# Where the gate decays are subtracted, and when a head's last transposes are issued, in a fused hybrid layer

## The chip, the core and the metric

One core of a Trainium2 chip. The core has five engines, each with a queue of its own that it works through in order: TensorE (PE, matrix multiply), VectorE (DVE), ScalarE (ACT), GpSimd (POOL) and SyncE (SP, which here only issues transfers). The metric is device time in microseconds, the median of a few runs.

## The reference

The kernel computes one decoder layer in float32 on 1024 positions of width 1024. All branch inputs come from one projection `z = h W_in` with `h = rmsnorm(x)`. Branch A is a chunked gated unit. Branch B, in which the change lies, is gated linear attention with 4 heads (key width 128, value width 256) in chunks of 64 positions:

```python
log_a = log_sigmoid(b_lr @ w_a2 + b_a2) / 16
b = cumsum(log_a within a chunk);  b_last = b[63];  b_ref = b[31]
qe = q * exp(b - b_ref);  ke = k * exp(b_ref - b)
o_intra = tril(qe ke^T) v
chunk_kv = (k * exp(b_last - b))^T v;  decay = exp(b_last)
state = decay * state + chunk_kv            # over the chunks
o = o_intra + (q * exp(b)) state_before
y = x + rmsnorm(concat(a_out, rmsnorm(o) * silu(b_gate)) @ W_out)
```

So each gate needs four exponentials: of b, of b less the middle of its chunk (d below) with both signs (the negative one is ke), and of the chunk's last value less b (f below).

## The kernel before, in words

Every float32 operand of a large product is split into a rounded high part and a low part (`split`, L106: a cast on ScalarE, L108, and a subtraction, L109, on VectorE or GpSimd), and a product is three matmuls (`mm3`, L114 to L116). The stages follow one another on TensorE: normalisation and the first projections (to about 72 us), the gated linear attention (about 72 to 316, with a tail), the projections of branch A, and the output projection.

For a head, `qk` (L441) runs over two halves of 512 positions. For each half `gates` (L394) makes the decays: one small matmul (L397), log-sigmoid in three ScalarE and two VectorE operations (L405 to L413), the cumulative sum b on VectorE (L415), d on VectorE (L420), f on GpSimd (L424), and four exponentials on ScalarE (ke L428, d L429, b L430, f L431), of which three overwrite their input. Then the key and query projections (`proj_col`) are multiplied by the four (L448 to L457), and the chunk products follow (`products`, L462). There are eight gates: four heads, two halves. After `qk`, a head projects its values and gates token tile by token tile (`proj_tok`), and `attend` (L485) makes the output of one tile: scaled on VectorE (L516, L520), two tiles together transposed on TensorE (L527), copied on ScalarE (L528), and after every fourth tile stored to `mix_d` by a transfer that GpSimd issues (L534).

What sets the order: closures are put off with `later(fn, n)` (L75); every four steps of a projection's inner dimension, `tick()` counts all of them down and issues those that are due. One such step is twelve matmuls of 512 columns. A tile pair's transposes (`out`, L522) are put off by 3 steps, the last pair of a head by 4 (L538); they then fall into the next head's `qk`, or, for the last head, into the projections of branch A. Within this program order a planner, which simulates the engines with a cost model, lays out each engine's queue: among the instructions that it believes ready it takes them by priority. So an edit in one place can change the queues of all engines. `issue_after(x)` makes the instructions of its block follow x on their engine. Tiles of a pool share their buffers in turn: f, b, d, ke and m have one buffer each, projection results take turns on eight PSUM banks. Between the projections and other work, the sums of `w_out` blocks for the output stage (`wout_sums`, L217) are made on VectorE (L230), from blocks loaded by SyncE, and stored back by it. After the last head, `vn` (L584) takes the memory of the closed pools; ScalarE evacuates the value projections into it (L656), and L662 transposes another weight in two banks.

Of the kernel before, what the change touches and what calls it, by code (L numbers as in the profile page):

```python
# [11 lines left out]
AF = mybir.ActivationFunctionType  # L12
ALU = mybir.AluOpType
PSUM = bass.MemoryType.PSUM

P = 128
S = 1024
D = 1024
NT = S // P
# [5 lines left out]
CH = 64  # L25
TAU = 16.0
# [7 lines left out]
def hybrid_layer(  # L34
# [16 lines left out]
    nc = tc.nc  # L51
    x, out = x[0], out[0]
# [16 lines left out]
    def bank():  # L69
        return psum.tile([P, 512], F32, tag="ps", name="ps")  # L70
# [4 lines left out]
    def later(fn, n=1):  # L75
        pending.append([n, fn])
# [19 lines left out]
    def rsqrt(dst, mean, more=None):  # L96
        if more is None:
            nc.gpsimd.tensor_scalar(out=dst, in0=mean, scalar1=EPS, scalar2=None, op0=ALU.add)
        else:
            nc.gpsimd.tensor_scalar(  # L100
                out=dst, in0=mean, scalar1=EPS, scalar2=more, op0=ALU.add, op1=ALU.add
            )
        nc.gpsimd.tensor_tensor(out=dst, in0=dst, in1=neghalf[:, : dst.shape[-1]], op=ALU.pow)


    def split(hi, lo, src, eng=None):  # L106

        cast = nc.scalar.copy(out=hi, in_=src)  # L108
        return cast, (eng or nc.vector).tensor_tensor(out=lo, in0=src, in1=hi.bitcast(F32), op=ALU.subtract)  # L109

    def mm3(ps, a, b, start, stop, goes_on=False):

        how = {"skip_group_check": True} if goes_on else {}
        nc.tensor.matmul(ps, a[0], b[0], start=start, stop=False, **how)  # L114
        nc.tensor.matmul(ps, a[0], b[1], start=False, stop=False, **how)  # L115
        nc.tensor.matmul(ps, a[1], b[0], start=False, stop=stop, **how)  # L116
# [217 lines left out]
    with tc.tile_pool(name="gla", bufs=1) as gp:  # L334
# [3 lines left out]
            out=causal, in_=causal, pattern=[[1, P]], base=0, channel_multiplier=-1,  # L338
# [11 lines left out]
        for i in range(4):  # L350
# [4 lines left out]
            out=w2[32:64], in0=w2_raw[32:64], in1=w2[32:64].bitcast(F32), op=ALU.subtract  # L355
# [8 lines left out]
        for r, w in enumerate(w_lr):  # L364
            nc.gpsimd.memset(w.bitcast(F32), 0.0)
            src = lr_raw[:, 4 * r : 4 * r + 4]
            for i in (0, 1, 3):
                nc.scalar.copy(out=w[:, :, 32 * i : 32 * i + RANK], in_=src)
            nc.gpsimd.tensor_tensor(
                out=w[:, :, 64 : 64 + RANK], in0=src, in1=w[:, :, 0:RANK].bitcast(F32), op=ALU.subtract  # L370
# [4 lines left out]
        for hf in range(2):  # L375
# [3 lines left out]
            for k in range(KT):  # L379
# [7 lines left out]
                out=lrT[96:128, c], in0=pl[96:128], in1=lrT[96:128, c].bitcast(F32), op=ALU.subtract  # L387
            )

        tt = nc.vector.tensor_tensor  # L390
# [3 lines left out]
        def gates(hd, hf):  # L394

            pz = bank()
            nc.tensor.matmul(  # L397
                pz, w2[:, hd * DK : (hd + 1) * DK], lrT[:, hf * 512 : (hf + 1) * 512],
                start=True, stop=True,
            )  # L400
            bias = ba[:, hd : hd + 1]

            f = gp.tile([P, 8, CH], F32, tag="f", name="f")
            sp = f.rearrange("p n c -> p (n c)")
            nc.scalar.activation(out=sp, in_=pz, func=AF.Abs, bias=bias)  # L405
            m = gp.tile([P, 8, CH], F32, tag="m", name="m")
            mf = m.rearrange("p n c -> p (n c)")
            nc.vector.tensor_scalar(
                out=mf, in0=pz, scalar1=bias, scalar2=0.0, op0=ALU.add, op1=ALU.min
            )  # L410
            nc.scalar.activation(out=sp, in_=sp, func=AF.Exp, scale=-1.0)
            nc.scalar.activation(out=sp, in_=sp, func=AF.Ln, bias=1.0)
            tt(out=mf, in0=mf, in1=sp, op=ALU.subtract)  # L413
            b = gp.tile([P, 8, CH], F32, tag="b", name="b")
            nc.vector.tensor_tensor_scan(  # L415
                out=b.rearrange("p n c -> p (n c)"), data0=seg, data1=mf, initial=0.0,
                op0=ALU.mult, op1=ALU.add,
            )
            d = gp.tile([P, 8, CH], F32, tag="d", name="d")
            tt(  # L420
                out=d, in0=b, in1=b[:, :, CH // 2 - 1 : CH // 2].to_broadcast([P, 8, CH]),
                op=ALU.subtract,
            )
            nc.gpsimd.tensor_tensor(  # L424
                out=f, in0=b[:, :, CH - 1 : CH].to_broadcast([P, 8, CH]), in1=b, op=ALU.subtract
            )
            ke = gp.tile([P, 8, CH], F32, tag="ke", name="ke")
            nc.scalar.activation(out=ke, in_=d, func=AF.Exp, scale=-1.0 / TAU)  # L428
            nc.scalar.activation(out=d, in_=d, func=AF.Exp, scale=1.0 / TAU)  # L429
            nc.scalar.activation(out=b, in_=b, func=AF.Exp, scale=1.0 / TAU)  # L430
            nc.scalar.activation(out=f, in_=f, func=AF.Exp, scale=1.0 / TAU)  # L431
            dec = gp.tile([P, LINE, 1], F32, tag="dec", name="dec", bufs=2)[:, 0:8]
            nc.vector.tensor_copy(dec, b[:, :, CH - 1 : CH])
            dec2 = gp.tile([P, LINE, 1], F32, tag="dec2", name="dec2", bufs=3)[:, 0:4]
            tt(out=dec2, in0=dec[:, 0::2], in1=dec[:, 1::2], op=ALU.mult)
            return b, d, f, ke, dec, dec2, m

        def parts(tag, shape, bufs):
            return [gp.tile(shape, F32R, tag=tag + i, name=tag + i, bufs=bufs) for i in "hl"]
# [45 lines left out]
        def attend(hd, t, got, v, sg, cur):  # L485

            qsp, kst, sc, dec2 = got[t // 4]
            j = t % 4
            po = bank()
            o = po[:, 0:DV]  # L490
            prev = cur.get("parts")
            if t < NT - 1:
                pn = bank()[:, 0:DV]
                mm3(pn, [k[:, j] for k in kst], v, True, True)
                if t == 0:
                    cur["st"] = gp.tile([P, DV], F32, tag="st", name="st")
                    nc.vector.tensor_copy(cur["st"], pn)
                else:
                    stt(
                        out=cur["st"], in0=cur["st"], scalar=dec2[:, j], in1=pn,  # L500
                        op0=ALU.mult, op1=ALU.add,
                    )
                cur["parts"] = parts("st", [P, DV], 2)
                split(*cur["parts"], cur["st"])
            mm3(o, [s[:, j] for s in sc], v, True, t == 0)
            if t > 0:
                mm3(o, [q[:, j] for q in qsp], prev, False, True)
            e = t % 2
            if e == 0:
                cur["og"] = gp.tile([P, 2, DV], F32, tag="og", name="og", bufs=2)  # L510
                cur["oss"] = gp.tile([P, LINE], F32, tag="oss", name="oss", bufs=2)[:, 0:2]
            og, oss = cur["og"], cur["oss"]
            nc.scalar.activation(
                out=og[:, e], in_=o, func=AF.Square, scale=DV ** -0.5, accum_out=oss[:, e : e + 1]
            )
            tt(out=og[:, e], in0=o, in1=sg, op=ALU.mult)  # L516
            if e == 1:
                rsqrt(oss, oss)
                for i in range(2):
                    nc.vector.tensor_scalar_mul(og[:, i], og[:, i], oss[:, i : i + 1])  # L520

                def out(t=t, og=og, mx=cur["mx"], hd=hd):  # L522
                    pt = bank()
                    ptv = pt.rearrange("p (e t c) -> p e t c", t=2, e=2)
                    for i in range(2):
                        for k in range(2):
                            nc.tensor.transpose(ptv[:, k, i], og[:, i, k * P : (k + 1) * P], ident)  # L527
                    nc.scalar.copy(  # L528
                        out=mx[:, :, (t - 1) * P : (t + 1) * P],
                        in_=pt.rearrange("p (e n) -> p e n", e=2),  # L530
                    )
                    if t % 4 == 3:
                        c = slice((t - 3) * P, (t + 1) * P)
                        nc.gpsimd.dma_start(  # L534
                            mix_d[2 * hd : 2 * hd + 2, :, c].rearrange("e p c -> p e c"), mx[:, :, c]
                        )

                later(out, 4 if t == NT - 1 else 3)  # L538

        def new_mix():  # L540
            return {"mx": slot_b([P, 2, S])}
# [5 lines left out]
        def first(t, got=got, cur=cur):  # L547
            v = parts("v", [P, DV], 2)
            split(*v, v0[:, t], nc.gpsimd)
            attend(0, t, got, v, sg0[:, t], cur)  # L550
# [38 lines left out]
    with tc.tile_pool(name="sgu", bufs=1) as sp_:  # L589
# [38 lines left out]
        def third_sum_h(k):  # L628
# [8 lines left out]
            out=wsr, in_=wsr, pattern=[[0, G], [-1, P]], base=0, channel_multiplier=1,  # L637
# [11 lines left out]
        for i in range(2):  # L649
            if i == 1:  # L650
                blk = block_a(((C_V + 512, 512),))
            for n, t in enumerate(range(NT) if i == 0 else (4, 5, 6, 7, 0, 1, 2, 3)):
# [5 lines left out]
                if (i, n) == (0, 4):  # L658
                    for r in range(2):
                        pt = bank()  # L660
                        for g in range(4):
                            nc.tensor.transpose(pt[:, g * P : (g + 1) * P], wsr[:, 4 * r + g], ident)  # L662
                        nc.scalar.copy(
                            out=wsT[:, 4 * r : 4 * r + 4], in_=pt.rearrange("p (g c) -> p g c", g=4)
# [5 lines left out]
                if (i, n) == (1, 2):  # L670
                    ones = wide()[:, 0:P]
                    nc.vector.memset(ones, 1.0)
                    for r in range(2):
# [5 lines left out]
                        for g in range(4 * r, 4 * r + 4):  # L679
                            nc.vector.scalar_tensor_tensor(  # L680
                                out=q[:, g], in0=pt[:, (g % 4) * P : (g % 4 + 1) * P],
# [328 lines left out]
```

## Time and profile before

| | us |
|---|---|
| median of 3 runs | 776.02 (773.84 to 777.74) |
| the profiled execution's own time | 775.63 |
| its span, first to last instruction | 773.9 |
| TensorE busy | 753.5 (97%) |
| VectorE busy | 499.8 (65%) |
| ScalarE busy | 389.3 (50%) |
| GpSimd busy | 131.2 (17%) |

The granted TensorE clock is 0.999 of full speed over the span. Busy shares are of one execution; an engine's idle time matters only where the engine that sets the end waits for it. In rows, L424 is line 424 of the kernel; PE, DVE, ACT, POOL and SP are the engines, and a q behind a name is its queue.

### The profile page before, as it was taken

The numbers are of one execution on the slowest core, as the hardware profiler recorded it, in microseconds if no ns is written. First come the engines' busy times: TensorE is split into PE (matmuls) and PEld (weight loads), VectorE is DVE, ScalarE is ACT, GpSimd is POOL, SyncE is SP. The second block draws the span as 40 slices with busy tenths as digits, with TensorE's granted clock in tenths as the row PEclk, the third lists the DMA queues.
The fourth block names the chain that finished last, engine by engine and source line by source line (L and its number), as shares of the span: only waits on it lengthen the run. The fifth ranks groups of instructions, "written<-read, shape, count | busy, mean of one in ns | idle before, by whom it ended". The sixth has DMA issues, their size and how long they took to land.

```text
span 773.9 us, 10106 instructions
## 1 busy us (share of the span) xinstructions
PE 753.5 (97%) x3680; PEld 622.8 (80%) x3680; DVE 499.8 (65%) x865; ACT 389.3 (50%) x680; POOL 131.2 (17%) x173
## 2 busy tenths in 40 slices
PE   6999999999999999999999999999999999999996
PEld 3787788787888888888878888888888788888885
DVE  4756689856666575654897289565565587534665
ACT  5635567637364746434442237556655652434431
POOL 2225144422222222322100000000000100000043
PEclk9999999999999999999999999999999999999999
DMA  9545520243622462343121012111211696346157
GB/s 293 182 135 177 170 76 1 83 177 121 199 82 83 154 220 72 107 162 112 57 80 28 0 55 55 55 54 55 55 54 55 206 356 226 109 164 244 56 217 272
DMA packets 79412, 97.87 MB, mean 126 GB/s; under 512 B 5569, under 2 KB 62913, under 8 KB 79362
## 3 DMA queue, kind: packets, MB, share of 16 engines
q1 hardware_dynamic: 75760, 87.64, 34.4%
q0 software_dynamic: 2480, 8.01, 3.3%
q10 hardware_dynamic: 1122, 1.58, 0.6%
q8 instruction: 29, 0.48, 0.3%
q14 instruction: 21, 0.17, 0.1%
HBM read 72.04 MB, written 25.17 MB: 126 GB/s over the span
## 4 chain that ended last, share of the span: by engine, by line
PE 74%; DVE 8%; DMA 6%; ACT 6%; issue 2%; POOL 1%; SPq 1%; DVEq 0%; POOLq 0%; ACTq 0%
PE ps L114 24%; PE ps L116 24%; PE ps L115 23%; DMA wb<-in_w_out_dram 3%; DMA wo_d<-wb 3%; PE ps L702 2%; DVE wb L230 1%; DVE wb L109 1%; DMA raw<-in_w_in_dram 1%; POOL f L424 1%; SPq L227 1%; ACT wh L108 1%; PE ps L527 1%; DVE og L520 1%; DVE stl L109 1%
## 5 line engine op out<-in xcount | busy, mean ns | idle before, releaser
L114 PE MATMUL ps<-gr,hT 128*128 128x512 f32 x384 | 152.3, 399 | 5.0 <-ACT hT L108 3.9
L116 PE MATMUL ps<-gr,hT 128*128 128x512 f32 x384 | 150.4, 393 | 0.0
L115 PE MATMUL ps<-gr,hT 128*128 128x512 f32 x384 | 150.2, 393 | 0.0
L109 DVE TENSOR_TENSOR gr<-raw,gr 128x1024 fp32r<-128x1024 f32 (+1 forms) x97 | 91.2, 961 | 22.9 <-ACT gr L108 22.3
L114 PE MATMUL ps<-hT,gr 128*128 128x512 f32 x256 | 100.3, 394 | 0.7 <-ACT u L775 0.7
L115 PE MATMUL ps<-hT,gr 128*128 128x512 f32 x256 | 100.0, 391 | 0.0
L116 PE MATMUL ps<-hT,gr 128*128 128x512 f32 x256 | 99.1, 393 | 0.0
L108 ACT CAST gr<-raw 128x1024 fp32r<-128x1024 f32 (+1 forms) x97 | 78.9, 838 | 36.8 <-PE ps L116 18.3
L114 PEld LDWEIGHTS ps<-gr,hT 128*128 128x128 f32 x384 | 72.8, 190 | 20.3 <-ACT hT L108 4.5
L116 PEld LDWEIGHTS ps<-gr,hT 128*128 128x128 f32 x384 | 72.7, 189 | 15.5 <-DVE hT L109 0.9
L114 PE MATMUL ps<-gr,ah 128*128 128x512 f32 x216 | 84.0, 389 | 0.0
L115 PE MATMUL ps<-gr,ah 128*128 128x512 f32 x216 | 84.0, 389 | 0.0
L115 PEld LDWEIGHTS ps<-gr,hT 128*128 128x128 f32 x384 | 72.8, 190 | 13.8
L116 PE MATMUL ps<-gr,al 128*128 128x512 f32 x216 | 81.4, 389 | 0.0
L114 PEld LDWEIGHTS ps<-hT,gr 128*128 128x128 f32 x256 | 48.1, 188 | 10.3 <-ACT u L775 1.2
L116 PEld LDWEIGHTS ps<-hT,gr 128*128 128x128 f32 x256 | 48.1, 188 | 10.2 <-DVE gr L109 0.2
L115 PEld LDWEIGHTS ps<-hT,gr 128*128 128x128 f32 x256 | 48.1, 188 | 9.6
L230 DVE TENSOR_TENSOR wb<-wb 128x256 f32<-128x256 f32 x64 | 28.8, 450 | 39.7 <-DMA wb<-in_w_out_dram 38.9
L115 PEld LDWEIGHTS ps<-gr,ah 128*128 128x128 f32 x216 | 40.5, 188 | 8.5
L114 PEld LDWEIGHTS ps<-gr,ah 128*128 128x128 f32 x216 | 40.5, 188 | 8.5
L116 PEld LDWEIGHTS ps<-gr,al 128*128 128x128 f32 x216 | 40.5, 188 | 8.3
L108 ACT CAST ah<-a 128x512 fp32r<-128x512 f32 x38 | 23.3, 622 | 46.7 <-PE ps L115 44.9
(232 smaller groups left out, 1323.5 us busy)
## 6 DMA issues: line engine op xcount, KB each, us to landing
raw<-in_w_in_dram SPq DMA_DIRECT2D x78, 256.0 KB, 3.2
gr<-wo_d SPq DMA_DIRECT2D x16, 1024.0 KB, 4.8
wb<-in_w_out_dram SPq DMA_DIRECT2D x64, 128.0 KB, 2.5
wo_d<-wh SPq DMA_DIRECT2D x16, 512.0 KB, 2.8
wo_d<-wb SPq DMA_DIRECT2D x16, 512.0 KB, 2.9
raw<-in_w_out_dram SPq DMA_DIRECT2D x12, 512.0 KB, 3.9
mix_d<-mixB POOLq DMA_DIRECT2D x8, 512.0 KB, 3.1
raw<-in_w_in_dram SPq DMA_DIRECT2D x8, 512.0 KB, 3.7
```

The costliest lines, as they stand in the source:

```text
L108: cast = nc.scalar.copy(out=hi, in_=src)
L109: return cast, (eng or nc.vector).tensor_tensor(out=lo, in0=src, in1=hi.bitcast(F32), op=ALU.subtract)
L114: nc.tensor.matmul(ps, a[0], b[0], start=start, stop=False, **how)
L115: nc.tensor.matmul(ps, a[0], b[1], start=False, stop=False, **how)
L116: nc.tensor.matmul(ps, a[1], b[0], start=False, stop=stop, **how)
L227: nc.sync.dma_start(b[:, i], w_out[(row + j) * P : (row + j + 1) * P, c : c + 256])
L230: sub = lambda out, a, c: nc.vector.tensor_tensor(out=out, in0=a, in1=c, op=ALU.subtract)
L424: nc.gpsimd.tensor_tensor(out=f, in0=b[:, :, CH - 1 : CH].to_broadcast([P, 8, CH]), in1=b, op=ALU.subtract)
L520: nc.vector.tensor_scalar_mul(og[:, i], og[:, i], oss[:, i : i + 1])
L527: nc.tensor.transpose(ptv[:, k, i], og[:, i, k * P : (k + 1) * P], ident)
L702: nc.tensor.matmul(pt[:, c], part[:, c], wsT[:, g], start=True, stop=True)
```

## The change

f's subtraction moves from GpSimd to VectorE, behind d's. Of the four exponentials ke's is issued first and the other three are held behind it, in the order of the program f, d, b. And `out` of a head's last tile pair is put off by 5 steps where it was 4.

```diff
-            nc.gpsimd.tensor_tensor(
-                out=f, in0=b[:, :, CH - 1 : CH].to_broadcast([P, 8, CH]), in1=b, op=ALU.subtract
-            )
+            tt(out=f, in0=b[:, :, CH - 1 : CH].to_broadcast([P, 8, CH]), in1=b, op=ALU.subtract)
             ke = gp.tile([P, 8, CH], F32, tag="ke", name="ke")
-            nc.scalar.activation(out=ke, in_=d, func=AF.Exp, scale=-1.0 / TAU)
-            nc.scalar.activation(out=d, in_=d, func=AF.Exp, scale=1.0 / TAU)
-            nc.scalar.activation(out=b, in_=b, func=AF.Exp, scale=1.0 / TAU)
-            nc.scalar.activation(out=f, in_=f, func=AF.Exp, scale=1.0 / TAU)
+            first = nc.scalar.activation(out=ke, in_=d, func=AF.Exp, scale=-1.0 / TAU)
+            with tc.issue_after(first.ins):
+                nc.scalar.activation(out=f, in_=f, func=AF.Exp, scale=1.0 / TAU)
+                nc.scalar.activation(out=d, in_=d, func=AF.Exp, scale=1.0 / TAU)
+                nc.scalar.activation(out=b, in_=b, func=AF.Exp, scale=1.0 / TAU)
...
-                later(out, 4 if t == NT - 1 else 3)
+                later(out, 5 if t == NT - 1 else 3)
```

`tt` is `nc.vector.tensor_tensor`.

## Rows read from the trace of the kernel before

**Rows 1.** The page, busy us by engine, share of the span, instructions.

```profile
PE 753.5 (97%) x3680; PEld 622.8 (80%) x3680; DVE 499.8 (65%) x865; ACT 389.3 (50%) x680; POOL 131.2 (17%) x173
```

**Rows 2.** TensorE's waits: us in total, times, longest us.

```profile
PE ps L527 <- DVE og L520: 1.8, 1, 1.8
PE ps L114 <- ACT gr L108: 1.1, 1, 1.1
PE ps L466 <- DVE d L454: 0.8, 1, 0.8
PE ps L114 <- ACT vh L108: 0.5, 1, 0.5
PE ps L468 <- DVE b L456: 0.4, 1, 0.4
```

**Rows 3.** Busy us of PE, PEld, DVE, ACT, POOL in the gate work's stretch.

```profile
72.00:316.00 244.00, 238.85 (x1318) 198.09 (x1317) 168.51 (x313) 144.10 (x262) 72.59 (x81) 1.00 0.38 123
```

**Rows 4.** Lines L424 and L420 (ns, least/median/most), and who waited for L424.

```profile
L424 POOL TENSOR_TENSOR f<-b x8: 1043/1746/2785, 82.4 to 303.2; 128x512 f32<-128x512 f32 x8
  ACT f L431: 9.1, 5
L420 DVE TENSOR_TENSOR d<-b x8: 679/1034/1529, 82.3 to 304.1; 128x512 f32<-128x512 f32 x8
```

**Rows 5.** Timeline by engine before TensorE's wait at 143.43: start, us, what.

```profile
137.95 2.79 POOL L424 TENSOR_TENSOR f<-b 128x512 f32<-128x512 f32 x1 [3.31 <-ACT mixB L528]
...
137.70 1.20 DVE L109 TENSOR_TENSOR gr<-raw,gr 128x1024 fp32r<-128x1024 f32 x1
139.15 0.69 DVE L420 TENSOR_TENSOR d<-b 128x512 f32<-128x512 f32 x1
...
140.77 0.63 ACT L431 ACTIVATE f<-f 128x512 f32<-128x512 f32 x1 [1.53 <-POOL f L424]
141.31 0.62 ACT L428 ACTIVATE ke<-d 128x512 f32<-128x512 f32 x1
141.83 0.61 ACT L430 ACTIVATE b<-b 128x512 f32<-128x512 f32 x1
142.34 1.03 ACT L108 CAST gr<-raw 128x1024 fp32r<-128x1024 f32 x1
```

**Rows 6.** Timeline before TensorE's wait at 181.61, and an L520 pair elsewhere.

```profile
180.34 1.07 POOL L424 TENSOR_TENSOR f<-b 128x512 f32<-128x512 f32 x1 [1.38 <-DVE b L415]
...
180.43 1.40 DVE L520 TENSOR_SCALAR og<-og,oss 128x256 f32<-128x256 f32 x2
182.13 0.68 DVE L420 TENSOR_TENSOR d<-b 128x512 f32<-128x512 f32 x1
...
181.61 0.44 PE L527 MATMUL ps<-ident,og 128*128 128x128 f32 x2 [1.76 <-DVE og L520]
...
286.24 0.62 DVE L520 TENSOR_SCALAR og<-og,oss 128x256 f32<-128x256 f32 x2 [0.63 <-POOL oss L103]
```

**Rows 7.** Timeline at head 1's last transposes, then behind the last head's.

```profile
210.61 0.60 PE L527 MATMUL ps<-ident,og 128*128 128x128 f32 x4
...
213.69 0.27 PE L466 MATMUL ps<-d,ke 128*64 128x64 f32 x1
...
370.75 0.59 ACT L528 COPY mixB<-ps 128x512 f32<-128x512 f32 x1 [7.45 <-PE ps L527]
378.84 2.32 ACT L656 ACTIVATE vn<-ps 128x256 f32<-128x256 f32 x8
...
373.75 0.71 POOL L534 DMA_DIRECT2D mix_d<-mixB  x1
...
384.22 1.03 PE L662 MATMUL ps<-ident,wsr 128*128 128x128 f32 x8
```

**Rows 8.** VectorE's waits for loads (total, times, longest), and one of them.

```profile
DVE wb L230 <- DMA wb<-in_w_out_dram: 38.9, 18, 5.4
...
87.22 0.42 DVE L230 TENSOR_TENSOR wb<-wb 128x256 f32<-128x256 f32 x1 [2.87 <-DMA wb<-in_w_out_dram]
```

## The prediction

> **What bounds the kernel now.** I read the busy shares first, then TensorE's own waits, then the stretches, and last the queues of VectorE, ScalarE and GpSimd around each TensorE wait. TensorE is busy 753.5 of 773.9 us [rows 1]: whatever the change does to another engine is worth only what it takes out of TensorE's idle time, or adds to it. The gate work (`gates`, `qk`, `attend`) runs from about 72 to 316 us; there TensorE is busy 238.85 of 244 us, so 5.15 us is all that this stretch holds [rows 3]. The list of TensorE's waits says where it lies [rows 2]: 1.8 us for a head's scaled output (`og`, L520, at 181.61), 1.1 us for a weight granule's cast (`gr`, L108, at 143.43), 0.8 and 0.4 us for the query products of head 0 (L454, L456, near 92), 0.5 us for a `v` cast near 268, and some 0.5 in shorter ones. The rest of TensorE's idle time is the start, the tail and short waits elsewhere, where no edited line runs. The other engines have room in the stretch (VectorE 168.5, ScalarE 144.1, GpSimd 72.6 of 244 us, rows 3), but they work through their queues in order, and that is how they hold TensorE up.
>
> **The change, part by part.**
>
> *f from GpSimd to VectorE.* Eight subtractions leave GpSimd, where they took 1.04 to 2.79 us, median 1.75 [rows 4]. On VectorE I price each by its twin, d's subtraction L420, of the same shape and form: 0.68 us when nothing runs beside it, 1.53 at worst [rows 4]. That adds 8 x 0.68 = 5.4 us to VectorE's queue. Something comes back: the eight L420 have a median of 1.03 us against the least of 0.68, so about 8 x 0.35 = 2.8 us were lost beside GpSimd's f. VectorE's net load is +2.6 us in 244, against some 75 us in which it is idle. Cover: TensorE's matmuls, which run on as long as no product or cast is late; without that cover it would cost the full 0.68 us per gate, 5.4 us in all. I take 0 for the load itself and keep 0 to +2.6 for the range.
>
> *ke's exponential first.* ScalarE waited five times, 9.1 us in total, at the head of its queue for GpSimd's f [rows 4], with the other exponentials and a cast stuck behind. After the change the first exponential needs only d. The one place where TensorE pays for this is 143.43 [rows 2, 5]: d was ready at 139.15 + 0.69 = 139.84, f only at 137.95 + 2.79 = 140.74, so f's exponential began at 140.77, then ke's at 141.31, b's at 141.83, and the cast that TensorE needs at 142.34. After: ke's starts at about 139.87 (0.03 behind its input, as f's did); f's subtraction ends on VectorE at 139.84 + 0.69 = 140.53, so f's exponential starts at 140.56, one more 0.52 later at 141.08, and the cast, with three exponentials ahead of it as before, at 141.60: 0.74 us earlier. If the planner puts all four ahead of it, it is at 142.12 and the gain is 0.2. If it puts the cast first, the whole 1.1 goes. I take 0.7, nearest to the order in the rows, and keep 0.2 to 1.1. What is late next is still that cast, by 0.4 us.
>
> *The same move at 181.61.* TensorE waited 1.76 us for the pair of L520. That pair took 1.40 us on VectorE from 180.43, beside GpSimd's f (180.34 to 181.41); another such pair, with GpSimd elsewhere, takes 0.62 [rows 6]. Without f on GpSimd the pair ends 0.8 us sooner, so long as the two subtractions stay behind it; d did (182.13). If f and d both go in front, the pair ends 2 x 0.68 - 0.8 = 0.6 us later than now. I take -0.8, the order of the rows, and keep -0.8 to +0.6. The Trainium skill (SBUF — State Buffer, "Who interferes with whom") says that VectorE and GpSimd share one port pair as an exclusive lock: of an operation in a two-port mode, or with two SBUF inputs, and a GpSimd operation that reads SBUF, the second to start is blocked until the first ends. By that rule the whole 0.8 goes with f; by the two durations alone the slow pair might have another cause and nothing need go. The trace is on the rule's side: the slow pair ends 0.42 us after GpSimd's f does. The same page's rule also speaks against the change, because the moved f has two SBUF inputs and can itself be blocked; it would then cost up to the 1.53 us of the slowest L420.
>
> *The other TensorE waits in the gates.* Near 92 VectorE had stood 2.87 us behind a `w_out` load (L230 at 87.22) and then carried the rest of its queue late into L454 [rows 8]; f has no part in that, so I take 0 for the 0.8 + 0.4. The `v` cast near 268 stands behind four ScalarE operations that were not waiting for f; 0, with 0.5 either way if the planner swaps them. The shorter ones: 0.
>
> *The last transposes one step later.* For each of the four heads' last pairs, four transposes, their copy (L528) and GpSimd's store to `mix_d` (L534) go from the fourth to the fifth step. A step is twelve matmuls: from head 1's transposes at 210.61 to the next step's products at 213.69 is 3.08 us, of which the transposes are about 0.4, so 2.7 us [rows 7]. TensorE doesn't wait for any of these four groups now, so nothing goes there. What is queued behind the later store on GpSimd is the next gate multiply or split; GpSimd idles over 70% of the stretch [rows 3]. In heads 1 and 2 the transposes now stand directly ahead of the products, and push them, and the next gate's start, some 0.4 us back; those chains gain about as much from the exponentials. The one place with a price is the last head: its copy (370.75) and store (373.75) release the memory into which ScalarE evacuates the next projections from 378.84 [rows 7]. Shifted by 2.7 us, that is 381.5. Eight operations of 256 columns were waiting there, so four banks were full; at 24 matmuls, or two steps, 5.4 us a bank, it is four and a half, and the two banks of L662 at 384.22 make it seven of eight. It costs nothing; it would cost up to 2.7 if the banks ran out. I take 0.
>
> Sum: -0.7 - 0.8 = -1.5 us on the profiled execution's 775.63 us (span 773.9 and 1.7 around it), 774.1. The median of the runs shown is 776.02, 0.4 above the profiled execution, and so I forecast 774.5 for the median.
>
> **The rivals.**
>
> *The stalls only move.* The order on every engine is planned anew. Speaking for it: five ScalarE waits of 9.1 us cost TensorE only 1.1 [rows 2, 4], so most of this time is covered already, and f ahead of L520 costs what the other place gains. The time is 776.0.
>
> *All of the gate stalls vanish.* An earlier chain in every gate could also let the casts and query products be placed better. Speaking against it: 0.8 + 0.4 hang on a load, not on f. Price: the 5.15 us of rows 3, 770.9.
>
> *Slower: a load's wait gets in front.* The sums of `w_out` (L230) stand in VectorE's queue wherever the planner thinks their loads have landed; they waited 38.9 us in 18 places, 5.4 at worst [rows 8]. Near 92 a wait of 2.87 gave TensorE stalls of 0.8 + 0.4, so some 1.6 us was covered. With more work on VectorE and every position planned again, the longest wait may come just ahead of L520 or of the products' inputs: 5.4 - 1.6 = 3.8 covered so much, 5.4 uncovered, say 4.6, with nothing gained elsewhere: 780.6. It decides from about 3.9 us uncovered. Against it: most of the 18 waits cost TensorE nothing now.
>
> *The handover runs out of banks,* by a later plan for the last transposes: +2.7 - 1.5, 777.2.
>
> **How the numbers follow.** Forecast 0.50, stalls only move 0.22, all vanish 0.10, a load's wait 0.14, handover 0.04. About 0.5% (3.9 us) is what a measurement can tell from no change. Below 772.1 lie the second rival and a little of the forecast's tail: faster 0.12. Above 779.9 lies the third: slower 0.13. The rest, 0.75, is the same. The range of 8 in 10 reaches from all vanished, 770.9, up to 778.6, which takes in the handover and the unknown VectorE load (776.0 + 2.6), and leaves out most of the load's wait. The shown runs alone spread from 773.84 to 777.74.
>
> **What would show it.** Right: no f on GpSimd; L420 at 0.68 throughout; ScalarE no longer waits for f but for d; the cast behind the exponentials about 0.7 us sooner and its TensorE wait at 0.4; the L520 wait at about 1.0; the last head's evacuation 2.7 us later without a TensorE wait. Wrong: a new TensorE wait over 1 us in the gates, above all behind L230, or both old ones unchanged.

## The result, and the profile after

The changed kernel takes 770.24 us (median of 6 runs, 769.3 to 772.23); the kernel before, beside it on the same chip, 775.09. The ratio is 0.9944 with a 95% interval of 0.9929 to 0.996: 0.56% or 4.3 us faster. The forecast was 774.5, and 770.24 lies under its range (770.9 to 778.6). Of the 4.3 us between forecast and result 0.9 is the start: the forecast began from a median of 776.02, and the six runs here have 775.09. The rest, 3.3, is the gain: 4.85 us by the two medians where 1.5 was expected. The profiled execution took 770.76 us, its span is 769.0, the mean granted clock 0.998 of full speed (0.999 before).

The page of the changed kernel, busy us by engine (answers to [rows 1]); then, of its list of TensorE's waits, the two that lie in the gate work ([rows 2]); then the stretch of [rows 3].

```profile
PE 752.5 (98%) x3680; PEld 622.8 (81%) x3680; DVE 497.5 (65%) x873; ACT 389.9 (51%) x680; POOL 119.1 (15%) x165
```

```profile
PE ps L475 <- DVE ks L450: 0.7, 1, 0.7
...
PE ps L114 <- ACT vh L108: 0.2, 1, 0.2
```

```profile
72.00:316.00 244.00, 243.09 (x1345) 202.50 (x1344) 171.54 (x327) 145.59 (x264) 61.98 (x74) 1.00 0.38 123
```

Of the five waits of [rows 2] four are gone and the fifth is down to 0.2 us, a new one of 0.7 has come, and TensorE's idle time in the stretch fell from 5.15 to 0.91 us. VectorE has eight instructions more, and yet its busy time over the span fell from 499.8 to 497.5 us.

The time that the gate work and the projections behind it take can be read without the start of the program, which varies by 1.9 us between the profiles of these kernels (60.78 to 62.69): from TensorE's first matmul for the gates' low-rank input (L381) to a wait that both kernels have in a later stage. The first fence is of the kernel before, the second of the changed one.

```profile
61.94 2.12 PE L381 MATMUL ps<-hT,w_lr 128*128 128x512 f32 x8 [0.65 <-POOL w_lr L369]
...
606.78 0.50 PE L114 MATMUL ps<-hT,gr 128*128 128x512 f32 x1 [0.73 <-ACT u L775]
```

```profile
62.42 1.89 PE L381 MATMUL ps<-hT,w_lr 128*128 128x512 f32 x7 [0.65 <-POOL w_lr L369]
...
601.87 0.50 PE L114 MATMUL ps<-hT,gr 128*128 128x512 f32 x1 [0.73 <-ACT u L774]
```

That is 606.78 - 61.94 = 544.84 us before and 539.45 after. I call it the marked time below; these are single profiled executions, so it supports a ratio but doesn't replace it. Here are the marked times of the kernel before, of the changed kernel and of f_five, a part of the change that comes below (length, then busy us of PE, PEld, DVE, ACT, POOL as in [rows 3]):

```profile
61.94:606.78 544.84, 538.96 (x2736) 448.46 (x2737) 362.03 (x665) 288.90 (x496) 94.32 (x113) 1.00 0.30 93
```

```profile
62.42:601.87 539.45, 537.81 (x2736) 448.31 (x2736) 359.94 (x673) 289.44 (x496) 82.05 (x105) 1.00 0.30 94
```

```profile
62.22:600.57 538.35, 536.80 (x2737) 448.26 (x2737) 360.11 (x673) 289.38 (x496) 82.13 (x105) 1.00 0.30 94
```

TensorE's idle time in it falls from 5.88 to 1.64 us, and its busy time from 538.96 to 537.81, although it does the same matmuls: 1.15 of the 5.39 us came out of what the profile counts as busy.

The two lines that now subtract on VectorE (duration ns least/median/most), and who waited for the first (answers to [rows 4]):

```profile
L420 DVE TENSOR_TENSOR d<-b x8: 676/684/691, 82.8 to 299.3; 128x512 f32<-128x512 f32 x8
...
  ACT ke L426: 4.8, 5
```

```profile
L424 DVE TENSOR_TENSOR f<-b x8: 674/684/686, 83.4 to 299.9; 128x512 f32<-128x512 f32 x8
```

All eight d now take the 0.68 us that was the least before, where four of the eight had taken 1.37 to 1.53; nobody waits for f. Around the place of the old wait at 143.43 ([rows 5]), changed kernel:

```profile
135.77 1.06 ACT L108 CAST gr<-raw 128x1024 fp32r<-128x1024 f32 x1
...
137.81 0.68 DVE L420 TENSOR_TENSOR d<-b 128x512 f32<-128x512 f32 x1
...
138.41 0.68 DVE L424 TENSOR_TENSOR f<-b 128x512 f32<-128x512 f32 x1
...
138.52 0.63 ACT L426 ACTIVATE ke<-d 128x512 f32<-128x512 f32 x1 [0.39 <-DVE d L420]
...
139.19 0.63 ACT L428 ACTIVATE f<-f 128x512 f32<-128x512 f32 x1
```

The cast stands ahead of ke's exponential now, not behind three of the four. And the pair of L520 (now L519) that made the wait at 181.61 ([rows 6]) stands ahead of the gate's scan, at 172.14:

```profile
172.14 0.62 DVE L519 TENSOR_SCALAR og<-og,oss 128x256 f32<-128x256 f32 x2
```

The last head's transposes, their copy and the evacuations into the released memory (answers to [rows 7]):

```profile
367.95 0.60 PE L526 MATMUL ps<-ident,og 128*128 128x128 f32 x4
...
368.59 0.59 ACT L527 COPY mixB<-ps 128x512 f32<-128x512 f32 x1 [10.18 <-PE ps L526]
...
376.94 2.32 ACT L655 ACTIVATE vn<-ps 128x256 f32<-128x256 f32 x8
...
379.32 1.03 PE L661 MATMUL ps<-ident,wsr 128*128 128x128 f32 x8
```

TensorE doesn't wait there. L661 comes 4.9 us sooner than L662 did, the copy only 2.16: the handover is 2.7 us later than the rest, as forecast, and free.

### The profile page after: what moved, and what is told of

It is laid out like the page before. It is cut to its first block, busy times and chain, and to the rows that moved or that the text cites. A ratio compares the mean times of both kernels' runs of the same rounds, so it can differ in the third digit from the quotient of the medians.

```text
span 769.0 us, 10126 instructions
## 1 busy us (share of the span) xinstructions
PE 752.5 (98%) x3680; PEld 622.8 (81%) x3680; DVE 497.5 (65%) x873; ACT 389.9 (51%) x680; POOL 119.1 (15%) x165
## 4 chain that ended last, share of the span: by engine, by line
PE 89%; DMA 3%; ACT 3%; DVE 2%; issue 1%; POOL 1%; SPq 0%; DVEq 0%; POOLq 0%; ACTq 0%
PE ps L114 28%; PE ps L116 28%; PE ps L115 28%; PE ps L701 2%; PE ps L381 1%; DMA raw<-in_w_in_dram 1%; DMA wo_d<-wb 1%; PE ps L526 1%; DMA wb<-in_w_out_dram 1%; PE ps L475 1%; PE ps L465 0%; PE ps L467 0%; DMA xt<-in_x_dram 0%; DVE wb L109 0%; DVE h L283 0%
## 5 line engine op out<-in xcount | busy, mean ns | idle before, releaser
L109 DVE TENSOR_TENSOR gr<-raw,gr 128x1024 fp32r<-128x1024 f32 (+1 forms) x97 | 91.2, 961 | 21.7 <-ACT gr L108 21.1
L115 PEld LDWEIGHTS ps<-gr,hT 128*128 128x128 f32 x384 | 72.9, 190 | 13.8
L230 DVE TENSOR_TENSOR wb<-wb 128x256 f32<-128x256 f32 x64 | 28.9, 452 | 36.2 <-DMA wb<-in_w_out_dram 35.5
```

The lines of the kernel that those rows point to most:

```text
L230: sub = lambda out, a, c: nc.vector.tensor_tensor(out=out, in0=a, in1=c, op=ALU.subtract)
```

## The experiments

Each kernel ran five rounds beside the kernel before. F stands for f's subtraction on VectorE, K for ke's exponential first, V for step five. The ratios of the parts together; the expectations and the readings follow by group. The ratios are to the kernel before on the same chip, whose median there was 774.15 to 775.09.

| kernel | edits | median us | ratio to before (95%) | mean ns of an L420 |
|---|---|---|---|---|
| kernel before | none | 775.09 | 1 | 1088 |
| five_only | V | 775.12 | 1.0013 (1.0004 to 1.0022) | 1298 |
| kefirst_only | K | 773.66 | 0.9993 (0.9984 to 1.0003) | 1192 |
| kefirst_five | K V | 773.59 | 0.9990 (0.9976 to 1.0003) | 1298 |
| sq_first | another order, below | 774.28 | 0.9995 (0.9983 to 1.0006) | 1192 |
| f_only | F | 770.07 | 0.9949 (0.9933 to 0.9965) | 683 |
| decays_four | F K | 771.32 | 0.9966 (0.9953 to 0.9979) | 685 |
| changed kernel | F K V | 770.24 | 0.9944 (0.9929 to 0.9960) | 684 |
| f_five | F V | 768.92 | 0.9926 (0.9913 to 0.9940) | 684 |
| after_twice | F K V + GpSimd reads | 772.77 | 0.9984 (0.9974 to 0.9995) | 1298 |
| after_write | F K V + GpSimd fills | 770.59 | 0.9946 (0.9931 to 0.9960) | 684 |
| f_five_twice | F V + GpSimd reads | 772.37 | 0.9972 (0.9960 to 0.9984) | 1297 |

The last column parts the kernels in two: none with L420 above 1000 ns is below 0.997, none with 683 to 685 above 0.9966. Within each part it says nothing: the kernel before, at 1088, is no faster than kefirst_five at 1298.

### The parts, first group

I suspected first that the gain came from the queues that the planner laid out anew (the moved cast and pair, "order theory"). five_only is V alone, kefirst_five K and V, decays_four F and K, f_five F and V.

```diff
# V
-                later(out, 4 if t == NT - 1 else 3)
+                later(out, 5 if t == NT - 1 else 3)
# K
-            nc.scalar.activation(out=ke, in_=d, func=AF.Exp, scale=-1.0 / TAU)
+            first = nc.scalar.activation(out=ke, in_=d, func=AF.Exp, scale=-1.0 / TAU)
+            with tc.issue_after(first.ins):
...
# F
-            nc.gpsimd.tensor_tensor(
+            tt(out=f, in0=b[:, :, CH - 1 : CH].to_broadcast([P, 8, CH]), in1=b, op=ALU.subtract)
```

> The kernel before with one edit: the last transposes of a head at five steps. f stays on GpSimd, the exponentials keep their order. Order theory (the TensorE waits went because the planner laid out the queues anew, and the step of the last transposes decides where the L520 pair stands): the wait of 1.76 us before the transposes of head 1's second pair is gone, the 1.13 us for the cast near 143 stays; 1.9 us faster than before (a wait costs some 0.15 more than its row). Theory of the prediction (the gain comes from GpSimd's f: port and ScalarE's wait): both waits stay, 0 us, L420 still at up to 1.5 us.

> The changed kernel with its step put back to four: f on VectorE and ke's exponential first. Order theory: the cast near 143 stands ahead of the exponentials, so that wait is gone (1.3 us); the L520 pair still stands behind the next gate's cumulative sum, so its wait stays, shorter by what the port costs, at 1.0 to 1.8 us; 1.3 to 2.1 us faster. Theory of the prediction: 0.7 and 0.8 less, 1.5 us faster, the cast's wait at 0.4 and the pair's at 1.0.

> f on VectorE and the step at five, but the exponentials without an order of their own. Order theory: the pair's wait gone; the cast stands behind ke's exponential alone, some 1.9 us sooner than before, so its wait is gone or under 0.2; 3.0 to 3.2 us faster. Theory of the prediction: 1.5 us faster (0.8 by the port, 0.7 at the cast), nothing from the step.

> ke's exponential first and the step at five, but f's subtraction stays on GpSimd. Order theory: both waits gone, as in the changed kernel, 3.0 to 3.2 us faster than before and within 0.7 us of the changed kernel, though L420 still takes up to 1.5 us beside GpSimd's f. Theory of the prediction: ScalarE still waits for GpSimd's f behind ke's, the port still blocks; 0 to 0.9 us faster.

In this form the order theory fell. five_only is 0.13% slower, which neither expectation had; f_five gains 5.7 us where the theories had at most 3.2 and 1.5, decays_four 2.6 where they had at most 2.1 and 1.5. In five_only the pair's wait at 181.61 and the cast's are gone, and two others have come, by its list of TensorE's waits:

```profile
PE ps L115 <- DVE stl L109: 1.6, 2, 1.0
PE ps L114 <- ACT vh L108: 1.6, 2, 1.1
```

In kefirst_five too both old waits are gone, and it is no faster than the kernel before by more than the noise. Its timeline shows what is late instead, near 184:

```profile
178.03 1.05 POOL L424 TENSOR_TENSOR f<-b 128x512 f32<-128x512 f32 x1 [5.82 <-DVE b L415]
...
178.10 1.53 DVE L420 TENSOR_TENSOR d<-b 128x512 f32<-128x512 f32 x1
...
179.66 0.63 ACT L428 ACTIVATE ke<-d 128x512 f32<-128x512 f32 x1 [3.07 <-DVE d L420]
...
183.36 0.37 ACT L108 CAST vh<-ps 128x256 fp32r<-128x256 f32 x1
...
183.78 0.39 PE L114 MATMUL ps<-vh,ksth 128*128 128x256 f32 x1 [1.40 <-ACT vh L108]
```

GpSimd's f and VectorE's d both start right behind the same scan; d ends 0.55 us behind f, having taken 1.53 instead of 0.68; ke, for which nothing else is missing, waits for d, the `v` cast behind the exponentials comes late, and TensorE waits 1.40. So ke first helps ScalarE little as long as f's subtraction delays ke's own input. It does help some: beside step five, without F, the ratio goes from 1.0013 to 0.9990, 1.5 us by the medians on the same chip.

decays_four keeps the pair where it was and tests the prediction's price for it. TensorE's list has

```profile
PE ps L526 <- DVE og L519: 1.0, 1, 1.0
```

where the prediction's step had 1.76 - 0.8 = 1.0 (the row itself says 0.98).

### f alone, ke alone, and the lock put back

The second group asked whether f's place alone makes the gain, and why. f_only is F alone, kefirst_only K alone. after_twice is the changed kernel in which GpSimd makes f's subtraction again, into a tile that nothing reads:

```diff
+            scr = gp.tile([P, 8, CH], F32, tag="scr", name="scr")
+            nc.gpsimd.tensor_tensor(
+                out=scr, in0=b[:, :, CH - 1 : CH].to_broadcast([P, 8, CH]), in1=b, op=ALU.subtract
+            )
```

sq_first leaves the kernel's parts as they were before and, for the gates that heads 1 and 2 make ahead for the next head, holds the ScalarE work behind the sum of squares of the tile before (L513), for which the pair of L520 had waited:

```diff
-            nc.scalar.activation(
+            cur["sq"] = nc.scalar.activation(
...
-                        ahead = gates(hd + 1, 0)
+                    with tc.issue_after(cur["sq"].ins):
+                        ahead = gates(hd + 1, 0)
```

> The kernel before with f's subtraction alone on VectorE; exponentials in their old program order, step at four. Theory A (f's place makes the gain, through GpSimd's slow f, its port and the waits behind it; the other two edits only choose where the rest lies): 3 to 4 us faster than before, L420 at 0.68, the L520 pair's wait left at about 1.0, the cast's wait gone. Theory B (f pays only together with the step of five, whose new waits near 184 and 193 it removes): about 1.5 us faster, as in the prediction.

> The kernel before with ke's exponential first and nothing else. Theory A: nothing, within 1 us of before: the cast's wait near 143 goes because the cast now stands ahead of the exponentials, but GpSimd's f stays in every gate and other waits take its place. Theory B: the cast's wait goes and nothing comes for it, 1.3 us faster.

> The changed kernel, and GpSimd makes the same subtraction a second time into a tile that nobody reads (work of no use to the result). The queues of TensorE, ScalarE, VectorE and SyncE are those of the changed kernel but for one pair of neighbours swapped. Port theory (GpSimd's operation beside VectorE's is the cost): L420 and L424 are held up to 0.9 us per gate again, TensorE waits come back, 2 to 4 us slower than the changed kernel. Order theory (the changed queues are the gain, GpSimd's work costs nothing by itself): within 0.5 us of the changed kernel, 4.3 us faster than before. Waiting theory (ScalarE's wait for GpSimd's f): also near the changed kernel, since f's exponential no longer waits for GpSimd, only b's does.

> The kernel before, and only ScalarE's work of the next head's early gate (L405 to L431) is held behind the sum of squares (L513) of the tile before it, for heads 1 and 2. If the pair's wait at 181.61 comes from that sum standing behind the log-sigmoid and its table loads in ScalarE's queue, that wait is gone with f still on GpSimd: 1.5 to 1.9 us faster, unless the later gate makes a new wait as in the run with five steps alone (then 0 to 1 us). If it comes from GpSimd's f beside the pair, the wait stays.

F alone gives 0.9949, as much as all three within the intervals. K alone takes away the cast's wait at 143.43 but not the pair's, and its 0.9993 can't be told from no change. sq_first takes away the wait at 181.61, the longest of [rows 2], and gains nothing that can be told either (0.9995): a wait of 0.8 for another pair of L520 stands at 193. Removing one wait by order is worth little; what shortens the chain in front of all of them is worth 4 us. The parts don't add up, though: F is worth 0.0051 alone, 0.0027 beside K, 0.0046 beside K and V, and 0.0087 beside V.

after_twice shows the cause. Its PE and SP queues are the changed kernel's, row for row, and VectorE's and ScalarE's differ in one swapped pair of neighbours each; nobody waits for the extra tile. L420 in it, and VectorE and GpSimd in the last gate, where each engine's rows stand by themselves:

```profile
L420 DVE TENSOR_TENSOR d<-b x8: 679/1527/1531, 81.3 to 303.1; 128x512 f32<-128x512 f32 x8
```

```profile
300.87 1.22 DVE L415 TENSOR_TENSOR_SCAN b<-seg,m 128x512 f32<-128x512 f32 x1
302.01 1.20 DVE L109 TENSOR_TENSOR gr<-raw,gr 128x1024 fp32r<-128x1024 f32 x1
303.13 1.53 DVE L420 TENSOR_TENSOR d<-b 128x512 f32<-128x512 f32 x1
```

```profile
302.17 1.94 POOL L426 TENSOR_TENSOR scr<-b 128x512 f32<-128x512 f32 x1 [2.64 <-DVE b L415]
```

The two take turns. GpSimd's subtraction starts at 302.17, beside VectorE's L109; at its least it takes 1.04 us, here it ends at 304.11, 0.9 us after L109's end at 303.21. d, next on VectorE, ends 0.55 us behind that, at 304.66. The Trainium skill (SBUF — State Buffer, "Who interferes with whom") calls the shared port pair an exclusive lock on which the second to start fully blocks; these rows agree, 1.53 against 0.68 us for d and 1.94 against 1.04 for the subtraction. TensorE pays for it in several places, by its list in after_twice:

```profile
PE ps L469 <- DVE d L457: 1.1, 1, 1.1
PE ps L114 <- ACT vh L108: 1.1, 2, 0.9
PE ps L530 <- DVE og L523: 0.8, 2, 0.5
...
PE ps L479 <- DVE ks L454: 0.6, 1, 0.6
```

Not all of this list is the lock's price. The first wait, 1.1 us, stands at 92.11, where VectorE had waited for a load:

```profile
86.48 0.42 DVE L230 TENSOR_TENSOR wb<-wb 128x256 f32<-128x256 f32 x1 [2.40 <-DMA wb<-in_w_out_dram]
```

The d of that gate took 0.69 us, and its f, 1.53, was done before VectorE stood idle; this is the wait near 92 that the prediction put down to a load, and it comes and goes between runs of one kernel. The 0.6 for `ks` is 0.7 in the changed kernel too. What is new behind the slow d is 0.9 for the `v` cast at 184.64, 0.5 and 0.3 for pairs of L520 (now L523), 0.3 for `stl` and 0.2 for a `gr`. In the stretch of [rows 3] TensorE idles 4.28 us in after_twice, 1.2 of it near 92, against 0.91 in the changed kernel.

The ratio falls back from 0.9944 to 0.9984, 3.1 us.

### Does the same pay for GpSimd's other subtractions?

From the fastest kernel so far, f_five (here f_five_again), the low parts of the scores (f5_sc), of the queries (f5_qs) and of both (f5_both) move to VectorE, eight each:

```diff
# f5_qs
-                split(*[p.rearrange("p j c -> p (j c)") for p in qsp], qs.rearrange("p n c -> p (n c)"), nc.gpsimd)
+                split(*[p.rearrange("p j c -> p (j c)") for p in qsp], qs.rearrange("p n c -> p (n c)"))
# f5_sc
-                    split(*sc, scm, nc.gpsimd)
+                    split(*sc, scm)
```

> f on VectorE and the last transposes at step five, without ke's exponential first: the fastest kernel so far (0.9926), run again beside the next three. Port theory (GpSimd's f held VectorE's queue up, and TensorE through it): 0.992 to 0.995, some 769 to 771 us. A rival, that its lead of 0.2% over the changed kernel was chance: 0.9945 or above.

> The same, and the subtraction of the scores' split (8 of about 1.29 us on GpSimd, 128x512) moves to VectorE too. TensorE has only some 0.8 us of idle time left in the gates' stretch of the kernel it starts from. Port theory with TensorE as the bound: VectorE gets 8 x 0.7 = 5.4 us more and its rows beside GpSimd shorten, but there is nothing left to give back: 0.991 to 0.995, within 0.8 us of the kernel run beside it. Rival 'every two-input operation off GpSimd pays as f did': another 0.3 to 0.5%, 0.989 or less, some 766 us. Rival 'VectorE becomes late': the scores' low part waits behind VectorE's queue, TensorE waits for it some 0.5 us in each of eight halves: plus 4 us, 0.998.

> The same for the subtraction of the query split before the products (8 of about 1.28 us on GpSimd). Port theory with TensorE as the bound: 0.991 to 0.995. 'Every such operation pays': 0.989 or less. 'VectorE becomes late': it stands on the way from the query products to TensorE's next products, so TensorE waits for it: 0.996 to 0.998.

> Both subtractions on VectorE beside f. GpSimd then has in the gates little but v's split, sums of partial squares and transfers. Port theory with TensorE as the bound: 0.991 to 0.995. 'Every such operation pays': 0.986 or less, some 764 us. 'VectorE becomes late': 0.998 to 1.002, since VectorE carries 11 us more in these stretches.

Measured, in this order: 768.55 us, 0.9924 (0.9908 to 0.9940); 769.2, 0.9932 (0.9912 to 0.9952); 768.67, 0.9924 (0.9905 to 0.9943); 769.98, 0.9940 (0.9921 to 0.9959). None gains. In f5_both these operations take 0.68 and 0.75 us on VectorE against 1.29 and 1.28 on GpSimd, but TensorE's list in f_five_again has no more than 0.7 us in the gates (the first two rows), and in f5_both the query products near 92 wait again (the third), which by itself tells little, since that wait comes and goes with a load. That there is nothing left to give is argued from this list; what a better order could still take out of TensorE's busy time was not tried.

```profile
PE ps L115 <- DVE stl L109: 0.5, 1, 0.5
PE ps L114 <- ACT vh L108: 0.2, 1, 0.2
```

```profile
PE ps L464 <- DVE d L452: 0.9, 1, 0.9
```

### Reading or only being busy, and what ke first is worth

GpSimd in after_twice was also 12 us busier. after_write keeps it busy at the same places with almost no reading: a copy of one column behind b, and two fills. All other engines' queues are the changed kernel's, row for row. f_five_twice is f_five with the subtraction of after_twice; after_again and f_five_third are the changed kernel and f_five run beside each other.

```diff
+            scr = gp.tile([P, 8, CH], F32, tag="scr", name="scr")
+            seen = nc.gpsimd.tensor_copy(scr[:, 0, 0:1], b[:, 7, CH - 1 : CH])
+            with tc.issue_after(seen.ins):
+                nc.gpsimd.memset(scr, 0.0)
+                nc.gpsimd.memset(scr, 0.0)
```

> The changed kernel, and on GpSimd behind each b a copy of one column of it and two fills of an unread tile of 128x512 (some 0.55 us each by L365's), so that GpSimd is busy for 1.1 us or more where it was with f. Port theory (only an operation that reads memory beside VectorE's two-input ones holds it up): L420 stays at a median of 0.68 us, and the time that of the changed kernel, 0.993 to 0.996. 'GpSimd busy' theory (its later work comes late, whatever it does): 0.9975 to 0.9995, as the kernel with f's subtraction repeated (0.9984).

> The changed kernel beside f_five_third. If ke's exponential first costs: 0.994 to 0.9955, and slower than the other by 0.15 to 0.2%. If it does nothing: within 0.1% of it.

> f on VectorE and step five without ke's exponential first. 0.9915 to 0.9935 if the earlier two measurements hold (0.9926, 0.9924); beside the changed kernel 0.15 to 0.2% faster, or within 0.1% of it if the earlier lead was chance.

> f_five, with GpSimd repeating f's subtraction into an unread tile. TensorE's and ScalarE's queues differ in a few places from f_five's. Port theory: L420 back above a mean of 1.0 us, some 2 to 4 us slower than f_five, 0.995 to 0.998. If the 3.1 us belonged to the one order of the changed kernel: within 1 us of f_five, 0.994 or less.

after_write takes 770.59 us, 0.9946, the time of the changed kernel (after_again 770.52, 0.9945, 0.9931 to 0.9958). GpSimd is busier in it than in the kernel before:

```profile
PE 751.4 (98%) x3680; PEld 622.2 (81%) x3680; DVE 497.2 (65%) x873; ACT 390.3 (51%) x680; POOL 133.4 (17%) x189
```

and VectorE doesn't notice. In the last gate of after_write, GpSimd, then VectorE:

```profile
297.23 1.09 POOL L426 COPY scr<-b 128x1 f32<-128x1 f32 x1 [2.63 <-DVE b L415]
298.38 0.53 POOL L428 MEMSET scr<- 128x512 f32 x1
298.97 0.53 POOL L429 MEMSET scr<- 128x512 f32 x1
```

```profile
297.08 1.20 DVE L109 TENSOR_TENSOR gr<-raw,gr 128x1024 fp32r<-128x1024 f32 x1
298.19 0.68 DVE L420 TENSOR_TENSOR d<-b 128x512 f32<-128x512 f32 x1
298.80 0.68 DVE L424 TENSOR_TENSOR f<-b 128x512 f32<-128x512 f32 x1
```

The fills run beside d and f, and both keep 0.68 us. The copy, one element a partition, is held until L109 ends (it ends at 298.32, L109 at 298.28). By the same section of the Trainium skill an operation of GpSimd that only writes doesn't contend with a two-input one of VectorE; the fills agree. So a busy GpSimd costs nothing here that can be told, one that reads a long operand beside VectorE costs 3 us. f_five_twice agrees in another order: L420 at 1526 ns again, 772.37 us against f_five_third's 769.37 on the same chip (0.9972 against 0.9928).

f_five measured 0.9926, 0.9924 and 0.9928 (0.9915 to 0.9942), the changed kernel 0.9944 and 0.9945; beside each other 769.37 and 770.52. decays_four and f_only differ by 0.0017 in the same sense. K therefore costs about 0.15%, 1.2 us, where f is on VectorE; single intervals overlap, but all of these measurements agree. f_five, the change without ke first, is the fastest kernel of this study. Where K costs it the marked times show: TensorE is busy 537.81 and 537.93 us in the two profiles of the changed kernel, 536.63 to 536.80 in the three of f_five, and its idle time hardly differs (1.64 and 1.96 against 1.37 to 2.02). So the cost stands in TensorE's busy time, in the order of its queue or in waits too short to be listed; which of the two isn't settled.

Some of the lock is left in the changed kernel. The one steady difference in TensorE's waits is 0.7 us for `ks` (L450) near 126, where f_five's and f_only's have 0.5 for `stl`. Ahead of that `ks`, `dec` takes 0.72 us instead of the 0.15 of decays_four, beside a subtraction on GpSimd (in decays_four it is `ks` itself that takes 0.96 instead of 0.41); and in the next gate the scan itself takes 1.93 us, beside GpSimd's low part of the scores, where f_five's takes 1.22:

```profile
125.01 0.73 POOL L109 TENSOR_TENSOR vl<-mixB,vh 128x256 fp32r<-128x256 f32 x1
...
125.04 0.72 DVE L434 TENSOR_TENSOR dec<-dec 128x4 f32<-128x4 f32 x1
```

```profile
133.85 1.50 POOL L109 TENSOR_TENSOR scl<-scm,sch 128x512 fp32r<-128x512 f32 x1 [1.90 <-ACT sch L108]
...
134.51 1.93 DVE L415 TENSOR_TENSOR_SCAN b<-seg,m 128x512 f32<-128x512 f32 x1
```

That scan is as slow in all profiles with K, and among those without only in f_five_twice's. No run takes these two operations off GpSimd with K in place, so what they cost isn't shown.

## Why the prediction was wrong, point by point

*What bounds the kernel* was right about the place and wrong about the size. The gain lies in the gates, where TensorE's idle time fell from 5.15 to 0.91 us. But 5.15 us isn't "all that this stretch holds": between the marks 1.15 us came out of TensorE's busy time too, and f_five's marked time is 6.49 us shorter than the kernel before's, with 0.81 us still idle in the stretch. (Its three ratios make 5.6 to 5.9 us, their intervals reach from 4.5 to 7.1.) So the price of the second rival and the lower end of the range, 770.9, which rest on the 5.15, were no limit.

*f's load on VectorE, "I take 0 for the load itself and keep 0 to +2.6": this is the step that failed.* It saw the 2.8 us that L420 lost beside GpSimd, but set it off against the 5.4 us of the moved f as if both were load. (The 2.8 is from a median of 1.03 us that no L420 took: four took 0.68 to 0.69, four 1.37 to 1.53, together 3.3 us above the least.) In busy time the sum was already off: d fell from 8 x 1088 to 8 x 684 ns (-3.2 us), the scaled pairs L520 from 13.8 to 10.0 us, the scan rose by 1.3, f came to 5.5, in all -0.3; with the rest of the engine, 499.8 to 497.5. But busy time is not the measure either: kefirst_five has 497.6 us, the same, and no gain. What counts is that d stands in the chain that the gate waits for (scan, d, ke's exponential, products) and f doesn't: up to 0.85 us of delay on d in a gate is delay for ScalarE, for the casts queued behind the exponentials and for the products, while f's own 0.68 us stands beside ScalarE's ke. The prediction wrote "the shorter ones: 0" for those places and priced the lock at the pair alone. The lock costs 0.0040 of the time, 3.1 us (after_twice against the changed kernel; 3.4 us by the ratios of f_five_twice and f_five_third). The rest of F, from kefirst_five's 0.9990 to after_twice's 0.9984, is 0.0006 or 0.5 us, under what is measured. So it is in the changed kernel's order; in f_five's the rest, from five_only's 1.0013 to f_five_twice's 0.9972, is 0.0041 or 3.2 us, and no run shows what it is made of. The lock is F's main price in the changed kernel, not the only thing that F's place can do.

*ke's exponential first, -0.7:* mis-sized, and of the wrong sign beside F. The cast's wait at 143.43 goes altogether (the 1.1 of its bound), since the planner put the cast in front; but it goes in five_only and f_only as well, so it isn't K's own. Alone K gives 0.9993, which can't be told from nothing; beside V it gains 1.5 us, beside F, as in the changed kernel, it costs some 1.2.

*The pair at 181.61, -0.8:* the price was right, 0.98 us left in decays_four where 1.0 was forecast. It was overtaken by V.

*The last transposes, 0:* right for the handover (2.7 us later, no wait) and nearly right for V without F (1.0013, 1 us slower). With F, V is worth 0.0022 (decays_four to the changed kernel; 0.0023 from f_only to f_five), 1.7 us, though the single intervals overlap: with step five the pair stands ahead of the scan and its last 0.98 us goes as well; the rest isn't traced. The prediction followed the moved transposes and their store, but not the scaling that feeds them, which the new due time let the planner move too.

*The waits near 92, 0:* not f's doing, as said. They were 1.2 us before, 0 in the changed kernel's first profile, 0.4 in its second (0.21 + 0.16), 0.3 in five_only, 0 in kefirst_only. They follow a `w_out` load, for which VectorE waited 2.87 us before, 0.96 and 2.22 in the changed kernel's two profiles; some of the 5.15 us of [rows 3] was this chance.

*The rivals.* "All of the gate stalls vanish", at 0.10, came nearest (770.9). Its reason, a chain earlier in every gate, was the right one, though its price was too low a bound, as said; it should have been worked out from the rows of L420 by gate. "The stalls only move" is what K and V do without F, within 1 us. The load's wait didn't get in front: VectorE's waits for L230 fell from 38.9 to 35.5 us, and in this profile none reached TensorE.

```profile
DVE wb L230 <- DMA wb<-in_w_out_dram: 35.5, 18, 5.1
```

*The signs named in advance* held in part: L420 at 0.68 throughout, ScalarE waiting for d and not for f, the evacuation 2.7 us later without a wait, no new wait over 1 us. The cast's wait was to be 0.4 us and the pair's about 1.0; both are gone.

## What to carry to other kernels

Where an instruction's durations split into two groups, such as 0.68 and 1.53 us, look for the engine that runs beside it in the slow ones, and price the difference once per occurrence on the chain in which the slowed instruction stands, not as load of its engine and not only where a wait is listed. An operation that seems free on an idle engine isn't, if it slows the first link of a chain on a busy one; a copy of it into an unread tile puts its price back by itself. The idle time of the bound engine is no sure limit of the gain, since part of what its rows call busy can go too. And one such move that pays doesn't mean that the next does: after f, two more gained nothing.

## What the runs showed of the hardware

- A GpSimd copy of one column (128x1) took 186 ns at least but a median of 863 and up to 1097 beside VectorE; fills of 128x512 took 524 to 544 in the same gates. The rows of after_write, the first of the two fills:

```profile
L426 POOL COPY scr<-b x8: 186/863/1097, 81.2 to 297.2; 128x1 f32<-128x1 f32 x8
```

```profile
L428 POOL MEMSET scr<- x8: 524/527/531, 82.0 to 298.4; 128x512 f32 x8
```

- That short read delayed nothing measurable on VectorE: the eight L420 of that kernel took 678 to 695 ns. In the gate shown it had all but ended when d began; what it does when it starts first was not tried.
- The same 128x512 subtraction of two operands takes 0.68 us on VectorE and at its least 1.04 us on GpSimd: the idle engine was the slower place for it in any case.
- VectorE operations beside a reading GpSimd, other than d: the scan of 128x512 took 1.93 us against 1.22 beside the low part of the scores, and an operation as small as `dec`'s 128x4 0.72 against 0.15 beside that of `v`.
